# Hybrid decoder layer on one core: query passes 512 wide, top-k behind the heads, softmax as its own step

## The chip, the cores and the metric

One Trainium2 chip, one core of it. The metric is the device time of one execution in microseconds, the median of the runs shown. The kernel is written in Tile: a planner that simulates the program fixes at compile time in which order each engine gets its instructions, by readiness and by the order of the program text, and sets the semaphores. Engines are PE (matrix), DVE (vector), ACT (scalar functions), POOL (GpSimd) and SP (issues DMAs).

## The reference, cut to what matters

```python
h2 = rms_norm(x, g_norm2) * (1 + sc2) + sh2            # 512 tokens x 1024
q = (h2 @ w_query).reshape(T, 8, 2, 128)               # 8 heads, 2 halves
s = einsum('thpd,pkd->thpk', q, sub_keys)              # 128 scores per half
s_top, i_top = top_k(s, 16)                            # first level
cand = s_top[:, :, 0, :, None] + s_top[:, :, 1, None, :]
best, pos = top_k(cand, 16)                            # second level
eidx = take_along(i0 * 128 + i1, pos); g = softmax(best)
a = gelu(einsum('thkd,td->thk', expert_u[eidx], h2))
out = einsum('thk,thkd->td', g * a, expert_v[eidx])    # 16384 experts x 1024
```

In front of it stand the attention and retention groups with their projections, behind it a residual and a last RMSNorm.

## The kernel before, in words

The 512 tokens are four blocks of 128 (`NB`). Blocks 0 to 2 (`DB`) take the expert layer densely: all 16384 experts in 128 chunks, `u_chunk` (line 746) for the inner products and GELU, then `v_load` and `v_mm` (lines 812, 833) for the weighted sum. Their gates are spread into a matrix G over experts by `g_steps` (line 773): 48 steps of four one-hot products on DVE (lines 784 to 787), 16 small matmuls on PE and two copies on ACT each. Block 3 (`GB`) gathers its 128 expert rows per token from HBM with indirect DMAs on POOL (`gather`, line 842).

Products in f32 precision are made of three matmuls (`mm3`, lines 80 to 83): a tile is split into a high part (ACT, line 76) and the rest (line 77, on DVE or POOL, as the caller says).

The order around the change:

- `ORDER` (line 45) lists the steps of the front, here its end: `h0 w1 q0 q1! h1 q2 q3`. `w` is the output projection of a pair of blocks (`wout`, 495), `h` the second norm and transpose of a pair (`h2`, 517), `q` the query of a pair for four heads (`query`, 552). A `!` gives a step high priority. In this stretch SP's DMAs keep the order of the text.
- `query` loads one 128-column piece of `w_query` per head and half, splits it (rest on POOL), makes 24 matmuls of 256 columns, copies the result (line 578), and a tile later makes the scores against the sub-keys (line 561), which are copied behind each head to `Sc` (line 564), over the residual buffers `blk`.
- Behind the front, for b in 0, 1, 2: the u chunks up to `UF[b]` (8 before block 1, 16 before block 2; rest of the split on POOL for chunks under 8, else DVE), then `topk(b)` (line 609). It calls `topk16` (lines 595 to 600) 16 times on 128 scores, adds the 50 candidates per head (lines 625 to 631), calls `topk16` 8 times on those, finds the indices with 16-way comparisons and trees (lines 645 to 655), makes the softmax (lines 656 to 665), and turns indices and gates with three PE transposes (lines 676 to 678).
- Then G steps and u chunks up to 32 alternate, chunks 32 to 35 come behind the last G matmul, and the last stage begins: a v chunk and a u chunk in turn, `R0` = 36 chunks apart. `topk(GB)` is issued at v chunk 2, behind the last one-hot product, and the gathers of block 3 follow in POOL's written order, between the splits of the v chunks.

Of the kernel before, what the change touches and what calls it, by code (L numbers as in the profile page):

```python
# [38 lines left out]
UF = {1: 8, 2: 16}  # L39
# [5 lines left out]
ORDER = "L m0! p1 d3 p2! m1 p3 d4 p4 d2 p5 p6 r0! r1! p7 r2 r3 X0 X1! d5! m2 g! m3 w0 X3 X2 h0 w1 q0 q1! h1 q2 q3"  # L45
# [3 lines left out]
def build(ctx: ExitStack, tc: tile.TileContext, A, out):  # L49
# [502 lines left out]
    def query(pr, hs):  # L552
        bs = (2 * pr, 2 * pr + 1)
# [4 lines left out]
        def scores():  # L558
            qs, h, q, p4 = pend.pop()
            for i in range(2):  # L560
                T.matmul(p4[:, i, q, :], qs[:, i * 128:(i + 1) * 128], subk[:, q, :], start=True, stop=True)
            if q:
                for i, b in enumerate(bs):
                    S.activation(Sc[b][:, h], p4[:, i], AF.Copy)

        for h in hs:
            p4 = acc().rearrange("p (b q k) -> p b q k", b=2, q=2)
            for q in range(2):
                raw = raw_t()
                G.dma_start(raw, A["w_query"][2 * h + q])  # L570
                hi, lo = split(raw, P)
                pa = acc()
# [5 lines left out]
                S.activation(qs[:, :256], pa[:, :256], AF.Copy)  # L578
                if pend:
                    scores()  # L580
                pend.append((qs, h, q, p4))
# [10 lines left out]
    eidx = cp.tile([128, 128], I32, name="eidx")  # L592
    gsm = cp.tile([128, 128], F32, name="gsm")

# [14 lines left out]
    def topk(b, after=None):  # L609
        v1 = tk.tile([128, 8, 2, 16], F32, name="v1", bufs=1)  # L610
        i1 = tk.tile([128, 8, 2, 16], U32, name="i1", bufs=1)
        for h in range(8):
            for q in range(2):
                topk16(v1[:, h, q, :], i1[:, h, q, :], Sc[b][:, h, q, :], 128)
# [5 lines left out]
        cd = tk.tile([128, 8, NC_], F32, name="cd", bufs=1)  # L620
        va, vb = v1[:, :, 0, :], v1[:, :, 1, :]
        o = 0
        for a in range(5):
            n = 16 // (a + 1)
            V.tensor_add(cd[:, :, o:o + n], vb[:, :, :n], va[:, :, a:a + 1].to_broadcast([128, 8, n]))
            o += n
        V.tensor_add(cd[:, :, o:o + 6].rearrange("p h (a b) -> p h a b", a=3),
                     vb[:, :, None, :2].to_broadcast([128, 8, 3, 2]),
                     va[:, :, 5:8, None].to_broadcast([128, 8, 3, 2]))
        o += 6  # L630
        V.tensor_add(cd[:, :, o:o + 8], va[:, :, 8:16], vb[:, :, 0:1].to_broadcast([128, 8, 8]))
        bst = tk.tile([128, 8, 16], F32, name="bst", bufs=1)
        bpos = tk.tile([128, 8, 16], U32, name="bpos", bufs=1)
        for h in range(8):
            topk16(bst[:, h], bpos[:, h], cd[:, h], NC_)
# [19 lines left out]
        tree(ij[:, 1], tm, V)  # L655
        nm = tk.tile([128, 8], F32, name="nmx", bufs=1)
        V.tensor_copy(nm, bst[:, :, 0])
        ee = bst
        V.tensor_sub(ee, bst, nm[:, :, None].to_broadcast([128, 8, 16]))
        S.activation(ee, ee, AF.Exp)  # L660
# [372 lines left out]
```

## Time and profile before

| | us |
|---|---|
| median of 3 runs (lowest to highest) | 1602.66 (1601.04 to 1605.63) |
| the profiled execution, its own time | 1607.23 |
| span of its records | 1605.2 |
| mean granted clock of TensorE | 0.983 of full speed |

Busy shares of the span: PE 94%, weight loads 86%, DVE 80%, POOL 53%, ACT 39%. The profile has one record per instruction; the views used are the page, tables of busy time by stretch, waits, groups by line, and the order in time of one engine. Busy times of neighbouring instructions overlap a little, so a rate is read from start to start.

### The profile page before, as it was taken

The page shows a single profiled execution, that of the slowest core. Times are in us where ns is not written, and L with a number is a line of the kernel's source. Part 1 is how long each engine was busy: PE and PEld are TensorE (multiplying, and loading weights), DVE is VectorE, ACT ScalarE, POOL GpSimd, SP SyncE. Part 2 cuts the span into 40 slices and gives each one's busy share as a digit, 9 for nine tenths or more (in the row PEclk, how much of TensorE's full clock was granted, in tenths as well). Part 3 has the DMA queues.
Part 4 walks back from the last instruction along what each step waited for, and adds up shares of the span by engine and source line. Part 5 has one row for each costly group of instructions (what it writes and reads, how often), then busy time and mean ns, then how long its engine had stood idle before and what let it go on. Part 6 is the DMA issues. An engine that isn't in the chain of part 4 may idle for free.

```text
span 1605.2 us, 24249 instructions
## 1 busy us (share of the span) xinstructions
PE 1515.3 (94%) x8977; PEld 1372.7 (86%) x8977; DVE 1289.7 (80%) x2338; ACT 629.8 (39%) x1015; POOL 849.6 (53%) x498
## 2 busy tenths in 40 slices
PE   7899999998899996999999999999999999999997
PEld 6788987797899995898888999999999999997885
DVE  6865754639989999999898987887887887888953
ACT  4433244444334554443233333333333333333432
POOL 0332742776440000138778877777687777765513
PEclk9999999999899998899999999999999999999998
DMA  9555440554333777959989999889898898899942
GB/s 355 183 186 173 134 159 29 183 163 139 106 118 113 247 234 217 286 185 332 326 312 324 317 333 320 314 305 324 316 330 293 315 322 329 313 321 343 323 159 77
DMA packets 196040, 395.62 MB, mean 246 GB/s; under 512 B 12241, under 2 KB 111569, under 8 KB 195922
## 3 DMA queue, kind: packets, MB, share of 16 engines
q1 hardware_dynamic: 157906, 257.22, 47.6%
q0 software_dynamic: 36864, 134.23, 23.7%
q10 hardware_dynamic: 1152, 2.62, 0.4%
q8 instruction: 70, 1.15, 0.3%
q14 instruction: 48, 0.39, 0.1%
HBM read 364.15 MB, written 29.88 MB: 245 GB/s over the span
## 4 chain that ended last, share of the span: by engine, by line
PE 29%; DMA 20%; issue 20%; DVE 15%; POOL 14%; ACT 1%; POOLq 0%; SPq 0%; DVEq 0%; ACTq 0%
POOL grow L844 8%; DMA grow<-in_expert_v_dram,eidx 8%; DMA grow<-in_expert_u_dram,eidx 6%; POOL vlo L77 5%; PE acc L82 4%; PE acc L81 4%; PE acc L83 4%; DMA vraw<-in_expert_v_dram 3%; PE ab L83 2%; PE ab L81 2%; PE ab L82 2%; DVE lo L77 1%; DMA raw<-in_wadaT_dram 1%; DVE junk L852 1%; DVE ohs L785 1%
## 5 line engine op out<-in xcount | busy, mean ns | idle before, releaser
L77 POOL TENSOR_TENSOR vlo<-vraw,vhi 128x1024 fp32r<-128x1024 f32 x92 | 242.0, 2631 | 293.3 <-ACT vhi L76 291.9
L76 ACT ACTIVATE hi<-raw 128x1024 fp32r<-128x1024 f32 x204 | 216.3, 1060 | 390.2 <-PE ab L82 245.2
L83 PE MATMUL ab<-hh,lo 128*128 128x384 f32 x1024 | 345.9, 338 | 3.6 <-DVE lo L77 2.6
L81 PE MATMUL ab<-hh,hi 128*128 128x384 f32 x1024 | 345.7, 338 | 0.7 <-ACT ga L758 0.6
L82 PE MATMUL ab<-hl,hi 128*128 128x384 f32 x1024 | 344.9, 337 | 0.0
L852 DVE SCALAR_TENSOR_TENSOR junk<-grow,h2n 128x1024 bf16<-128x1024 f32 x128 | 202.0, 1578 | 50.4 <-DMA grow<-in_expert_u_dram,eidx 47.5
L865 DVE SCALAR_TENSOR_TENSOR gacc<-grow,wsl,gacc 128x1024 f32<-128x1024 f32 x126 | 184.4, 1471 | 67.2 <-DMA grow<-in_expert_v_dram,eidx 66.9
L77 DVE TENSOR_TENSOR lo<-raw,hi 128x1024 fp32r<-128x1024 f32 x151 | 204.1, 1352 | 35.5 <-ACT hi L76 35.4
L844 POOL DMA_INDIRECT grow<-in_expert_u_dram,eidx x128 | 180.5, 1410 | 82.0 <-DVE junk L852 33.3
L844 POOL DMA_INDIRECT grow<-in_expert_v_dram,eidx x128 | 190.6, 1489 | 56.7 <-DVE gacc L865 27.8
L83 PEld LDWEIGHTS ab<-hh,lo 128*128 128x128 f32 x1024 | 192.4, 188 | 6.9 <-DVE lo L77 4.6
L81 PEld LDWEIGHTS ab<-hh,hi 128*128 128x128 f32 x1024 | 192.8, 188 | 4.5 <-ACT ga L758 1.0
L82 PEld LDWEIGHTS ab<-hl,hi 128*128 128x128 f32 x1024 | 192.7, 188 | 3.6
L77 POOL TENSOR_TENSOR lo<-raw,hi 128x1024 fp32r<-128x1024 f32 x53 | 133.0, 2512 | 105.4 <-ACT hi L76 104.2
L829 ACT ACTIVATE wh<-wf 128x384 fp32r<-128x384 f32 x110 | 57.5, 524 | 260.5 <-issue 220.8
L76 ACT ACTIVATE vhi<-vraw 128x1024 fp32r<-128x1024 f32 x110 | 115.5, 1050 | 57.2 <-DMA vraw<-in_expert_v_dram 55.0
L82 PE MATMUL acc<-vlo,wh 128*128 128x512 f32 x330 | 129.7, 394 | 6.1 <-POOL vlo L77 6.1
L83 PE MATMUL acc<-vhi,wl 128*128 128x512 f32 x330 | 128.5, 390 | 0.0
L81 PE MATMUL acc<-vhi,wh 128*128 128x512 f32 x330 | 123.2, 390 | 3.2 <-ACT wh L829 1.8
L81 PE MATMUL acc<-hi,hh 128*128 128x256 f32 (+2 forms) x296 | 91.6, 317 | 7.4 <-ACT hi L76 4.9
L830 DVE TENSOR_TENSOR wl<-wf,wh 128x384 fp32r<-128x384 f32 x110 | 88.0, 801 | 11.9 <-ACT wh L829 11.7
L82 PE MATMUL acc<-lo,hh 128*128 128x256 f32 (+2 forms) x296 | 93.8, 317 | 1.5 <-DVE lo L77 0.8
(339 smaller groups left out, 3303.3 us busy)
## 6 DMA issues: line engine op xcount, KB each, us to landing
raw<-in_uT_dram SPq DMA_DIRECT2D x128, 512.0 KB
vraw<-in_expert_v_dram SPq DMA_DIRECT2D x110, 512.0 KB
Gd<-stg SPq DMA_DIRECT2D x12, 2048.0 KB
gtl<-Gd SPq DMA_DIRECT2D x32, 768.0 KB
raw<-in_wadaT_dram SPq DMA_DIRECT2D x40, 512.0 KB
raw<-in_w_query_dram SPq DMA_DIRECT2D x32, 512.0 KB
raw<-in_expert_v_dram SPq DMA_DIRECT2D x18, 512.0 KB
raw<-in_w_out_dram SPq DMA_DIRECT2D x16, 512.0 KB
```

Source lines behind the costliest of these rows:

```text
L76: S.activation(hi[:, :n], raw[:, :n], AF.Copy)
L77: lo_engine.tensor_sub(lo[:, :n], raw[:, :n], hi[:, :n].bitcast(F32))
L81: T.matmul(o, wh, rh, start=start, stop=False, skip_group_check=skip)
L82: T.matmul(o, wh, rl, start=False, stop=False, skip_group_check=skip)
L83: return T.matmul(o, wl, rh, start=False, stop=stop, skip_group_check=skip)
L785: V.tensor_tensor(oh[1], io, bc(ij[:, 0]), op=OP.is_equal)
L829: S.activation(wh, wf, AF.Copy)
L830: V.tensor_sub(wl, wf, wh.bitcast(F32))
L844: P.indirect_dma_start(out=r, out_offset=None, in_=A[table], in_offset=bass.IndirectOffsetOnAxis(ap=eidx[:, s:s + 1], axis=0))
L852: V.scalar_tensor_tensor(jk, r, 1.0, h2n, op0=OP.mult, op1=OP.mult, accum_out=asl[:, s:s + 1])
L865: V.scalar_tensor_tensor(g, r, wsl[:, s:s + 1], g, op0=OP.mult, op1=OP.add)
```

## The change: what it does

The query runs heads 0 and 1 in passes of two blocks, then heads 2 to 4 and 5 to 7 for all four blocks in passes of 512 columns (`QS`); `h1` comes ahead of it. Scores are copied block by block and half by half. Behind each head `level1` makes its first-level calls for the blocks of the pass, block 3 among them; behind head 3 `level2(b, 0)` makes the second level of heads 0 to 3 of blocks 0 to 2. Values and indices of the first level have buffers of their own per block; `bst`, `bpos`, `cd` and the tile `ti` of four 128-column groups lie in `blk`. After the query, per block: the other half of the second level, `topk` (indices only), `gates` (softmax), u chunks up to `UF[b]`, now 2, 7, 12, then `topk_fin`, four transposes and two copies. Chunks 0 to 11 (`NPL`) have their rest made on POOL.

```diff
-UF = {1: 8, 2: 16}
+NPL = 12
+UF = {0: 2, 1: 7, 2: 12}
+QS = (((0, 1), (0, 1)), ((2, 3), (0, 1)), ((0, 1, 2, 3), (2, 3, 4)), ((0, 1, 2, 3), (5, 6, 7)))
-ORDER = "... w0 X3 X2 h0 w1 q0 q1! h1 q2 q3"
+ORDER = "... w0 X3 X2 h0 w1 h1 Q0 Q1 Q2 Q3"
...
         def scores():
-            qs, h, q, p4 = pend.pop()
-            for i in range(2):
-                T.matmul(p4[:, i, q, :], qs[:, i * 128:(i + 1) * 128], subk[:, q, :], start=True, stop=True)
+            qs, h, q = pend.pop()
+            p4 = acc()
+            for i in range(len(bs)):
+                cs = slice(i * 128, (i + 1) * 128)
+                T.matmul(p4[:, cs], qs[:, cs], subk[:, q, :], start=True, stop=True)
+            for i, b in enumerate(bs):
+                last["qa"] = S.activation(Sc[b][:, h, q], p4[:, i * 128:(i + 1) * 128], AF.Copy).ins
             if q:
-                for i, b in enumerate(bs):
-                    S.activation(Sc[b][:, h], p4[:, i], AF.Copy)
+                for b in bs:
+                    level1(b, h)
+                if h == H // 2 - 1:
+                    for b in DB:
+                        level2(b, 0)
...
-                    mm3(pa[:, :256], hi[:, ks], lo[:, ks], hh[:, bs[0]:bs[0] + 2, k, :],
-                        hl[:, bs[0]:bs[0] + 2, k, :], k == 0, k == 7)
+                    mm3(pa[:, :n], hi[:, ks], lo[:, ks], hh[:, bs[0]:bs[0] + len(bs), k, :],
+                        hl[:, bs[0]:bs[0] + len(bs), k, :], k == 0, k == 7)
...
+    def level1(b, h):
...
+        for q in range(2):
+            topk16(v1[:, h, q, :], i1[:, h, q, :], Sc[b][:, h, q, :], 128)
...
+    def level2(b, half):
+        bst, bpos, cd, _ = spare(b)
...
+        for a in range(5):
+            n = 16 // (a + 1)
+            V.tensor_add(cd[:, hs, o:o + n], vb[:, :, :n], va[:, :, a:a + 1].to_broadcast([128, 4, n]))
...
+        for h in range(4 * half, 4 * half + 4):
+            topk16(bst[:, h], bpos[:, h], cd[:, h], NC_)
...
+    def gates(b, after=None):
+        ti = tin[b]
+        ee = ti[:, 3].rearrange("p (h k) -> p h k", h=8)
+        with tc.issue_after(after) if after else ExitStack():
+            S.activation(ee, ee, AF.Exp)
...
+        gh = tk.tile([128, 16, 8], F16, name="pb", bufs=1).rearrange("p k h -> p (k h)")
+        V.tensor_scalar(gh, gg, GSC, None, op0=OP.mult)
+        V.scalar_tensor_tensor(ti[:, 3], gg, GSC, gh, op0=OP.mult, op1=OP.subtract)
+        V.tensor_copy(ti[:, 2], gh)
+
+    def topk_fin(b, after):
+        ti = tin[b]
+        with tc.issue_after(after):
             p = ob()
-            T.transpose(p[:, :128], iF[:, 0], ident)
-            T.transpose(p[:, 128:256], iF[:, 1], ident)
-            T.transpose(p[:, 256:384], gg, ident)
+            for q in range(4):
+                T.transpose(p[:, q * 128:(q + 1) * 128], ti[:, q], ident)
...
     for b in DB:
-        while nu < UF.get(b, 0):
-            u_chunk(nu, P if nu < 8 else V)
+        level2(b, 1)
+        topk(b)
+        gates(b, last["qa"])
+        while nu < UF[b]:
+            u_chunk(nu, P if nu < NPL else V)
             nu += 1
-        topk(b, last.get("u"))
+        topk_fin(b, last["u"])
...
             with tc.issue_after(last["o"]):
+                level2(GB, 0)
+                level2(GB, 1)
                 topk(GB)
+                gates(GB)
```

## Rows read from the trace of the kernel before

**Rows 1.** The page, part 1: busy us (share of the span) xinstructions

```profile
PE 1515.3 (94%) x8977; PEld 1372.7 (86%) x8977; DVE 1289.7 (80%) x2338; ACT 629.8 (39%) x1015; POOL 849.6 (53%) x498
```

**Rows 2.** Busy us by stretch (us from, to; length; engines; clock; DMA), last stage

```profile
700.00:800.00 100.00, 96.36 (x481) 85.49 (x480) 86.65 (x105) 32.27 (x44) 73.11 (x43) 1.00 0.86 300
800.00:1000.00 200.00, 195.69 (x991) 177.54 (x990) 180.04 (x206) 71.37 (x97) 157.68 (x90) 1.00 0.92 322
```

**Rows 3.** The same table, from the query to the G build's end

```profile
308.00:320.00 12.00, 11.23 (x91) 10.60 (x89) 4.22 (x5) 7.27 (x12) 10.83 (x8) 1.00 0.63 230
308.00:361.00 53.00, 52.23 (x441) 51.53 (x440) 19.33 (x104) 27.05 (x49) 40.52 (x20) 1.00 0.53 175
361.00:443.00 82.00, 67.76 (x521) 64.74 (x520) 80.84 (x370) 35.64 (x71) 45.77 (x19) 0.94 0.38 122
443.00:493.00 50.00, 48.27 (x276) 47.28 (x276) 42.84 (x147) 16.70 (x25) 15.48 (x6) 1.00 0.37 124
493.00:580.00 87.00, 85.69 (x687) 81.06 (x685) 86.03 (x192) 44.03 (x72) 0.00 (x0) 1.00 0.62 194
580.00:651.00 71.00, 53.32 (x543) 48.17 (x543) 69.09 (x113) 37.92 (x68) 0.00 (x0) 0.85 0.74 225
```

**Rows 4.** Waits of DVE, 308 to 651: us in total, times, longest

```profile
DVE v L596 <- ACT blk L564: 28.1, 7, 5.1
...
DVE i L597 <- PE ob L677: 3.0, 2, 2.2
```

**Rows 5.** DVE in order of time (start, us): first-level calls, last one-hot product

```profile
320.28 0.49 DVE L596 MAX8 v<-blk 128x8 f32<-128x128 f32 x2 [2.50 <-ACT blk L564]
...
322.44 0.29 DVE L600 FIND_INDEX8 i<-v,blk 128x8 uint32<-128x128 f32 x1
...
649.52 0.69 DVE L787 TENSOR_TENSOR ohs<-ohs,gt 128x1024 f16<-128x1024 f16 x1
```

**Rows 6.** DVE by line, 308 to 651 (five), then 652 to 711 (two): busy, mean ns

```profile
L77 DVE TENSOR_TENSOR lo<-raw,hi 128x1024 fp32r<-128x1024 f32 x25 | 30.7, 1229 | 6.0 <-ACT hi L76 6.0
L605 DVE TENSOR_TENSOR t4k<-t4k 128x1024 f16<-128x1024 f16 (+2 forms) x27 | 22.6, 860 | 0.2
...
L646 DVE TENSOR_TENSOR t4k<-t4k,dd 128x2048 f16<-128x2048 f16 x3 | 7.7, 2550 | 0.0
...
L537 DVE TENSOR_SCALAR w<-tp,mod 128x256 f32<-128x256 f32 x8 | 3.9, 531 | 0.0
L542 DVE TENSOR_TENSOR hl<-w,hh 128x256 fp32r<-128x256 f32 x8 | 3.9, 510 | 0.0
...
L605 DVE TENSOR_TENSOR t4k<-t4k 128x1024 f16<-128x1024 f16 (+2 forms) x9 | 4.0, 462 | 0.1
...
L646 DVE TENSOR_TENSOR t4k<-t4k,dd 128x2048 f16<-128x2048 f16 x1 | 1.2, 1204 | 0.0
```

**Rows 7.** DVE, then POOL, in order of time in topk(0)

```profile
388.15 0.18 DVE L625 TENSOR_TENSOR cd<-v 128x24 f32<-128x24 f32 x1
...
388.56 3.22 DVE L646 TENSOR_TENSOR t4k<-t4k,dd 128x2048 f16<-128x2048 f16 x1
...
388.12 5.91 POOL L77 TENSOR_TENSOR lo<-raw,hi 128x1024 fp32r<-128x1024 f32 x2 [1.70 <-ACT hi L76]
```

**Rows 8.** PE in order of time: 512 wide (output projection), score matmuls of the query

```profile
298.07 0.39 PE L81 MATMUL acc<-hi,hh 128*128 128x512 f32 x1
298.30 0.39 PE L82 MATMUL acc<-lo,hh 128*128 128x512 f32 x1
...
322.77 0.60 PE L561 MATMUL acc<-subk,w 128*128 128x128 f32 x4
...
326.05 0.61 PE L561 MATMUL acc<-subk,w 128*128 128x128 f32 x4
```

**Rows 9.** Waits of PE, 400 to 420

```profile
PE ob L676 <- DVE i L674: 9.6, 1, 9.6
```

**Rows 10.** POOL in order of time: the first gather

```profile
710.91 1.90 POOL L844 DMA_INDIRECT grow<-in_expert_u_dram,eidx  x1 [26.01 <-DVE eidx L670]
```

More of the change, by code (lines that the diff above doesn't have):

```diff
@@ L550, in h2, with query @@
                     S.dma_start(h2d[:, kp * 256:(kp + 1) * 256], hn[:, :256])
-    def query(pr, hs):
-        bs = (2 * pr, 2 * pr + 1)
+    def query(bs, hs):
+        n = len(bs) * 128
         for b in bs:
@@ L607, in tree, with spare, topk @@
         e.tensor_add(dst, t[:, 0], t[:, 1])
[L609 to L614, printed above, removed]
+    lv, tin = {}, {}
+    def level1(b, h):
+        if b not in lv:
+            if b == 1:
+                t = lv[0][2]
+            else:
+                t = (tk if b == GB else fr).tile([128, 512 if b == GB else 1024], F32,
+                                                 name=("fhi", None, "flo", "v1")[b], bufs=1)
+            o = 512 * (b == 1)
+            v = t[:, o:o + 256].rearrange("p (h q a) -> p h q a", h=8, q=2)
+            i = t[:, o + 256:o + 512].bitcast(U32).rearrange("p (h q a) -> p h q a", h=8, q=2)
+            lv[b] = v, i, t
+        v1, i1, _ = lv[b]
+        for q in range(2):
+            topk16(v1[:, h, q, :], i1[:, h, q, :], Sc[b][:, h, q, :], 128)
+    def spare(b):
+        f = blk[b].rearrange("p a c -> p (a c)")
+        return (f[:, 0:128].rearrange("p (h k) -> p h k", h=8),
+                f[:, 128:256].bitcast(U32).rearrange("p (h k) -> p h k", h=8),
+                f[:, 256:256 + H * NC_].rearrange("p (h n) -> p h n", h=8), f[:, 1024:1536])
+    def level2(b, half):
+        bst, bpos, cd, _ = spare(b)
+        v1 = lv[b][0]
+        hs = slice(4 * half, 4 * half + 4)
+        va, vb = v1[:, hs, 0, :], v1[:, hs, 1, :]
+        o = 0
+        for a in range(5):
+            n = 16 // (a + 1)
+            V.tensor_add(cd[:, hs, o:o + n], vb[:, :, :n], va[:, :, a:a + 1].to_broadcast([128, 4, n]))
+            o += n
+        V.tensor_add(cd[:, hs, o:o + 6].rearrange("p h (a b) -> p h a b", a=3),
+                     vb[:, :, None, :2].to_broadcast([128, 4, 3, 2]),
+                     va[:, :, 5:8, None].to_broadcast([128, 4, 3, 2]))
+        o += 6
+        V.tensor_add(cd[:, hs, o:o + 8], va[:, :, 8:16], vb[:, :, 0:1].to_broadcast([128, 4, 8]))
+        for h in range(4 * half, 4 * half + 4):
+            topk16(bst[:, h], bpos[:, h], cd[:, h], NC_)
+    def topk(b):
+        bst, bpos, _, ti = spare(b)
+        i1 = lv[b][1]
         di = tk.tile([128, 2, 17, 8], F16, name="di", bufs=1)
@@ L688, in mla_all @@
         mix_T(b, 0, mla(b))
+    last = {}
     yms = [None] * NB
@@ L729, in build @@
             h2(n)
-        elif o == "q":
-            query(n // 2, range(4 * (n % 2), 4 * (n % 2) + 4))
+        elif o == "Q":
+            query(*QS[n])
         hp.close()
@@ L737, in build @@
     gas = {}
-    last = {}
     def u_load(c):
@@ L874, in build @@
             left -= 1
-        u_chunk(c, P if c < 8 else V)
+        u_chunk(c, P if c < NPL else V)
     held = [u_load(c) for c in range(R0 - HOLD, R0 - HOLD + 3)]
@@ L886, in build @@
     row_bc(5, gt2)
+    eidx = lp.tile([128, 128], I32, name="eidx")
+    gsm = lp.tile([128, 128], F32, name="gsm")
     vacc += [acc() for _ in range(3)] + [tpb() for _ in range(2)] + [ob()]
```

52 lines of the change are left out of this document (15 added, 37 removed).

## The prediction

> **What bounds the kernel now.** I read four views, from coarse to fine. The page's first part: PE is busy for 1515 of 1605 us [rows 1], so the time of a stage is PE's work unless something starves it. The table of stretches shows where that happens. From 700 us on PE is busy for all but 8.0 us of 300 [rows 2], and that stage (u chunks and v chunks together) has a fixed amount of PE work: it ends a fixed time after it starts. So the question is when it starts. It waits for the last step of the G build, whose last one-hot product starts at 649.5 [rows 5], and the G build hangs on DVE: from 361 to 651 DVE is busy 80.8 of 82, 42.8 of 50, 86.0 of 87 and 69.1 of 71 us [rows 3], while PE stands idle for 17.7 us of the last of these. Ahead of that, from 308 to 361, the picture is turned round: PE is full (52.2 of 53) and DVE idles for 33.7 us. The waits of DVE say on what: 28.1 us on the copies of the query scores [rows 4]. All in all DVE is busy 298.1 of the 343 us from 308 to 651 and idle 44.9. So the start of the last stage moves by the change of DVE's work before 651, plus the change of its idle time. PE's share of the query is not the term.
>
> **The change, part by part** (on the start of the last stage, in us).
>
> *Block 3's first level comes forward.* Before, all of `topk(3)` ran behind the G build. Now its 16 first-level calls run behind the query heads. Two calls take from 320.28 to 322.65 including their last instruction, 2.4 us [rows 5], so one is 1.21 and 16 are **+19.4** on DVE ahead of 651. The other three blocks' calls only move.
>
> *Split engine.* `NPL` gives POOL the low halves of chunks 0 to 11 instead of 0 to 7: four fewer on DVE at 1.23 [rows 6], **-4.9**.
>
> *Second level in halves, softmax apart.* Seven additions of `cd` become fourteen per block, 21 more in three blocks. One took 0.18 [rows 7], so 21 are 3.8 at most, less where neighbours overlap. `gates` adds three small copies per block and drops one, some 2 in all. I take **+3** for both (bounds 1 and 6; near the middle, since back-to-back records overlap).
>
> *Query passes.* A 256-wide tile repeats every 3.27 us with its four score matmuls, which span 0.6 [rows 8]. A 512-wide matmul starts 0.23 after the one before it [rows 8], 24 of them take 5.6; with eight score matmuls a tile is 6.5, twice 3.27. So PE gains nothing: 8 x 3.27 + 12 x 6.5 = 104 us either way, against 32 x 3.27. Weight loads, splits (20 instead of 32) and loads of `w_query` (20 instead of 32, on SP) fall away where neither ACT nor the DMA engines were full: 27.1 of 53 us, share 0.53 [rows 3]. Score copies become 64 narrow ones on ACT for 32; even at 0.4 each they are 26 us in 104 and hide in ACT's idle half. I put all of this at nothing; without that cover it would be those 26 us.
>
> *DVE's idle time.* Built by hand from those periods, with `h2(1)` now ahead of the query. Up to 320 as before: 12.0 - 4.2 = 7.8 idle [rows 3] (the first call is at 320.28 [rows 5]). Q0 and Q1 are eight tiles, 26.2 us of PE, plus some 6 for the transposes of `h2(1)` and the wait for its last quarter: PE starts Q2 at 340. Meanwhile DVE has 16 first-level calls (19.4) and 7.8 of `h2(1)` (L537, L542) [rows 6], which now meets POOL's splits; I allow 4 for that, and DVE runs dry at 320 + 31 = 351. The first four-block head is complete after three tiles and its copies, 340 + 19.5 + 1 = 360.5: 9 idle. A head feeds DVE 8 x 1.21 = 9.7 per 13.0 of PE, so 3.3 more before the next one. Then the first half of the second level (three blocks, about 4.5 each) falls due behind head 3 and DVE has a backlog past the end of the query, near 418. That makes 20. Of the 11.2 idle after 361 before, the 3.0 in which an index tile waited for PE's transposes [rows 4] goes (each block has its own tile now), and I leave 6. So 26 for 44.9: **-19**. Bounds: 14 (always fed from 361 on) and 45 (nothing gained).
>
> *POOL beside DVE.* The second step of `topk` slows when POOL splits: L646 took 3.22 us at 388.56, beside two splits that took 5.91 [rows 7], and 1.2 after 652, where POOL stood mostly idle [rows 6]. In 308 to 651 the two largest groups carry 7.7 - 3 x 1.2 = 4.1 and 22.6 - 3 x 4.0 = 10.6 of such excess [rows 6]; with the smaller ones I estimate 25. Before, blocks 0 and 1 met splits of the query at 2.4 in 3.27 us; now only chunks 0 to 11 are beside block 0 and part of block 1, and the first halves of the second level run among splits every 6.5 us. I take **-4** (bounds: -25, none left; +10, four more splits at 2.4 in the way).
>
> The rule for this is on the Trainium skill's page SBUF — State Buffer, section "SBUF: two separate sides": a GpSimd instruction and a DVE instruction with two SBUF inputs exclude each other for a whole instruction. The rows of L646 agree; by the rule the loss goes with the number of splits that fall beside `topk`, about as many as before, which would make this term 0 instead of -4 and the sum 4 us worse.
>
> *Waits added.* `topk_fin` puts four transposes on PE behind the chunk that `UF` names. If DVE is late, the following chunks queue behind them, as for 9.6 us before [rows 9]. Each chunk's split waits in turn, but PE had 17.7 us to spare in 580 to 651 [rows 3], so a wait of that size costs nothing; beyond it, it counts in full. `Exp` in `gates` waits behind the last score copy on ACT, ahead of GELUs that have time.
>
> *Sum:* 19.4 - 4.9 + 3 - 19 - 4 = **-5.5**.
>
> *After the start.* The indices came so late that POOL, in its written order, stood 26.0 us in front of the first gather, at 710.9 [rows 10]. With 19.4 less to do there DVE gives the indices earlier, and v splits no longer pile up behind. PE idles 8.0 us in 700 to 1000 [rows 2]; I take half, **-4** (bounds 0 and -8).
>
> The profiled execution took 1607.23 us (span 1605.2), 4.57 above the median of the runs. 1607.2 - 9.5 = 1597.7; less 4.57 that is **1593** against 1602.66.
>
> **Rivals.**
>
> 1. *DVE is not fed earlier.* The place is the first four-block head: if its scores come late (Q1 waiting longer for `h2(1)`, or the planner putting heads behind other PE work), DVE's idle stays at 45 while block 3's 19.4 us are in front of the G build. Then 19.4 - 4.9 + 3 - 4 = +13.5, and +9.5 with the 4 behind the start: **1612**. It decides from about 40 us of idle on, since 14 more than my 26 is a loss of 4.8. For it: the wide pass doubles the time to a head's scores, and DVE before needed only 4.9 us a head. Against: the two heads in two-block passes give DVE 19.4 us of work to bridge this gap.
>
> 2. *POOL takes it back.* The loss beside POOL does not shrink by 4 but grows by 4 or 5, because `h2(1)`, the half levels and `topk` of two blocks all meet POOL's splits: 1593 + 9 = **1602**, no change. For it: 25 us lost that way before. Against: 40 splits in the query and chunks become 32.
>
> 3. *PE was bound by weights.* In 308 to 361 weight loads are busy 51.5 of 53 us [rows 3]. The wide passes need 480 instead of 768 of the query's loads, and with 2.8 us for 24 of them one costs at most 0.12: PE would gain up to 288 x 0.12 = 34 us, DVE's idle would fall to some 10 (the 7.8 up to 320 and little else), and it ends at 1593 - 16 = **1577**. That loads, not matmuls, measure TensorE is what the Trainium skill says (Perfetto Trace Analysis, "Identifying the Most-Contended Engine"). Against: 0.23 per 512-wide matmul is as long per column [rows 8].
>
> **How the numbers follow.** About 0.3%, 4.8 us, is what a measurement of this kernel can tell from no change. Forecast 0.49, rival 1 0.22, rival 2 0.23, rival 3 0.06. Faster: 0.49 + 0.06 = 0.55. Same 0.23. Slower 0.22. The forecast's own range is 1587 to 1598, from idle times of 20 to 30. The whole range reaches down to rival 3 and to contention nearly gone, 1577, and up to rival 1, 1612; what lies outside is both bad ends together (idle 45 and +10 beside POOL), or both good ends.
>
> **What would show it.** DVE's idle from the start of the query to the last one-hot product: 26, against 45. Block 3's first level ahead of that product, and the product near 645 instead of 650. Query tiles 6.5 us apart; PE waiting on DVE at least as long as before near the end of the G build. Two-input DVE instructions beside splits still at two to three times their length. First gather less than 40 us behind the last one-hot product, instead of 710.9 - 649.5 = 61. It is wrong if query tiles come much under 6.5, if DVE idles 40 or more, or if PE loses more time in the last stage than it did.

## The result, and the profile after

| | before | after |
|---|---|---|
| median of four runs, same chip | 1603.91 us (1601.04 to 1605.63) | 1587.53 us (1585.24 to 1613.96) |
| ratio, with 95% interval | | **0.9866** (0.9833 to 0.9899) |
| the same kernel on another chip (run 9) | 1609.80 us | 1592.16 us, 0.9901 (0.9881 to 0.9920) |
| profiled execution, span | 1607.23, 1605.2 us | 1585.5, 1583.7 us |

The ratio leaves out the one disturbed run of after, the 1613.96; the median of the other three is 1585.50. The kernel is faster: by 21 us by the first ratio, by 18 by these medians, by 16 by the second ratio. The forecast was 9.5 us. The page of after, part 1 (busy us, share of the span, instructions), beside [rows 1]:

```profile
PE 1507.8 (95%) x8692; PEld 1358.3 (86%) x8692; DVE 1276.3 (81%) x2369; ACT 622.1 (39%) x1027; POOL 824.2 (52%) x490
```

The table of stretches of after (us from, to; length; PE, PE's weight loads, DVE, ACT, POOL busy; clock; DMA), in the cuts of [rows 2, 3] as far as they are the same:

```profile
308.00:361.00 53.00, 47.67 (x321) 42.87 (x320) 34.02 (x171) 24.26 (x57) 29.63 (x14) 0.97 0.43 141
361.00:443.00 82.00, 82.00 (x434) 72.71 (x433) 77.12 (x524) 31.21 (x74) 33.74 (x14) 1.00 0.27 90
443.00:493.00 50.00, 36.26 (x184) 35.06 (x183) 49.62 (x146) 18.03 (x25) 16.27 (x6) 0.86 0.24 75
493.00:580.00 87.00, 85.89 (x722) 80.38 (x720) 84.84 (x137) 48.02 (x79) 0.00 (x0) 1.00 0.70 210
...
700.00:800.00 100.00, 100.00 (x510) 91.31 (x510) 93.95 (x109) 35.61 (x49) 77.67 (x46) 1.00 0.91 328
800.00:1000.00 200.00, 200.00 (x1021) 182.85 (x1020) 162.22 (x196) 71.41 (x98) 150.84 (x87) 1.00 0.88 311
```

DVE's idle time in 308 to 361 fell from 33.7 to 19.0 us. PE's idle time moved out of 361 to 443 into 443 to 493, where it stands behind DVE's top-k. And from 700 to 1000 PE has no gap at all, with 1531 matmuls in these 300 us where before had 1472 [rows 2].

The waits of DVE in after, 308 to 644 (us in total, times, longest), against [rows 4], and DVE in order of time, against [rows 5]:

```profile
DVE fhi L601 <- ACT blk L567: 13.3, 8, 4.0
DVE flo L601 <- ACT blk L567: 5.6, 4, 3.1
```

```profile
325.37 0.49 DVE L601 MAX8 fhi<-blk 128x8 f32<-128x128 f32 x2 [1.17 <-ACT blk L567]
...
642.68 0.68 DVE L826 TENSOR_TENSOR ohs<-ohs,gt 128x1024 f16<-128x1024 f16 x1
```

The waits on score copies are 18.9 us for 28.1. The last one-hot product starts at 642.7 instead of 649.5: 6.8 us of the 21.5 that the span lost. The other 14.7 lie behind it. The waits of PE in after, 644 to the end, are all that is left there, 2.8 us. The longest stands at 1428.8 us, far behind block 3's top-k:

```profile
PE acc L83 <- ACT ga L868: 1.9, 1, 1.9
PE ab L83 <- ACT gb L794: 0.5, 1, 0.5
PE acc L85 <- DVE wl L869: 0.4, 1, 0.4
```

And POOL in order of time shows the first gather 40.0 us behind that product, against [rows 10]: it waited 4.8 us instead of 26.0.

```profile
682.68 1.23 POOL L883 DMA_INDIRECT grow<-in_expert_u_dram,eidx  x1 [4.77 <-DVE eidx L705]
```

### The profile page after: what moved, and what is told of

Read it like the earlier page. It is cut to its first block, busy times and chain, and to the rows that moved or that the text cites. A ratio compares the mean times of both kernels' runs of the same rounds, so it can differ in the third digit from the quotient of the medians.

```text
span 1583.7 us, 23659 instructions
## 1 busy us (share of the span) xinstructions
PE 1507.8 (95%) x8692; PEld 1358.3 (86%) x8692; DVE 1276.3 (81%) x2369; ACT 622.1 (39%) x1027; POOL 824.2 (52%) x490
## 4 chain that ended last, share of the span: by engine, by line
PE 49%; DMA 16%; DVE 15%; issue 12%; POOL 8%; ACT 1%; SPq 0%; POOLq 0%; DVEq 0%; ACTq 0%
DMA grow<-in_expert_v_dram,eidx 8%; PE ab L85 6%; PE ab L83 6%; PE ab L84 6%; PE acc L83 5%; PE acc L85 5%; PE acc L84 5%; POOL grow L883 4%; DMA vraw<-in_expert_v_dram 4%; PE tp L85 2%; PE tp L84 2%; PE tp L83 2%; POOL vlo L79 2%; PE ob L85 1%; PE ob L84 1%
## 5 line engine op out<-in xcount | busy, mean ns | idle before, releaser
L83 PE MATMUL ab<-hh,hi 128*128 128x384 f32 (+2 forms) x1184 | 404.4, 342 | 7.0 <-ACT ga L794 6.5
L85 PE MATMUL ab<-hh,lo 128*128 128x384 f32 (+2 forms) x1184 | 403.8, 341 | 2.8 <-POOL lo L79 2.0
L84 PE MATMUL ab<-hl,hi 128*128 128x384 f32 (+2 forms) x1184 | 401.8, 339 | 0.0
L78 ACT ACTIVATE hi<-raw 128x1024 fp32r<-128x1024 f32 x192 | 203.7, 1061 | 405.5 <-PE ab L84 245.6
L891 DVE SCALAR_TENSOR_TENSOR junk<-grow,h2n 128x1024 bf16<-128x1024 f32 x128 | 193.2, 1509 | 64.2 <-DMA grow<-in_expert_u_dram,eidx 63.3
L79 DVE TENSOR_TENSOR lo<-raw,hi 128x1024 fp32r<-128x1024 f32 x147 | 212.3, 1445 | 32.9 <-ACT hi L78 32.8
L83 PEld LDWEIGHTS ab<-hh,hi 128*128 128x128 f32 x1184 | 224.1, 189 | 15.1 <-ACT ga L794 7.2
L85 PEld LDWEIGHTS ab<-hh,lo 128*128 128x128 f32 x1184 | 223.8, 189 | 8.0 <-POOL lo L79 2.4
L84 PEld LDWEIGHTS ab<-hl,hi 128*128 128x128 f32 x1184 | 224.0, 189 | 7.1
L883 POOL DMA_INDIRECT grow<-in_expert_u_dram,eidx x128 | 177.5, 1387 | 50.4 <-DVE junk L891 21.7
L79 POOL TENSOR_TENSOR lo<-raw,hi 128x1024 fp32r<-128x1024 f32 x45 | 110.5, 2456 | 146.9 <-ACT hi L78 146.8
L869 DVE TENSOR_TENSOR wl<-wf,wh 128x384 fp32r<-128x384 f32 x110 | 89.6, 814 | 13.2 <-ACT wh L868 12.0
```

Source lines behind the costliest of these rows:

```text
L78: S.activation(hi[:, :n], raw[:, :n], AF.Copy)
L79: lo_engine.tensor_sub(lo[:, :n], raw[:, :n], hi[:, :n].bitcast(F32))
L83: T.matmul(o, wh, rh, start=start, stop=False, skip_group_check=skip)
L84: T.matmul(o, wh, rl, start=False, stop=False, skip_group_check=skip)
L85: return T.matmul(o, wl, rh, start=False, stop=stop, skip_group_check=skip)
L869: V.tensor_sub(wl, wf, wh.bitcast(F32))
```

## The experiments

Theory for the gain behind the start: POOL works in its written order. Before, it stood 26 us in front of the first gather, the v splits queued behind it, and a v chunk came late in a stage that PE bounds. Rival: DVE's own load in block 3's top-k made the v chunks late. Theory for the start: DVE's work and idle time, as the prediction summed them. Rivals: the parts of the change taken singly.

Runs 1 to 4 shared a chip, 5 to 8 a second, 9 to 12 a third; a ratio is to the kernel before on the same chip. "Start" is the start of the last one-hot product. "Front" is the time to it from the last addition of the output projection on POOL, where the part that all kernels share ends. "Stage" is the time from the start to the end of the last matmul, "PE idle" PE's idle time in it, "low" the part of it in which TensorE's granted clock was 0.50, the lower of its two levels (1.2 and 2.4 GHz). "Matmuls" is PE's count in the first 400 us of the stage, "idle" DVE's idle time from 308 us to the start. All but the ratio are of the one profiled execution, which lies up to 6.5 us off the median of its kernel's runs (run 7).

| run | ratio (95%) | start | front | stage | PE idle | low | matmuls | idle |
|---|---|---|---|---|---|---|---|---|
| before | 1 | 649.5 | 340.0 | 944.1 | 13.0 | 3.4 | 1988 | 44.9 |
| after | 0.9866 (0.9833 to 0.9899) | 642.7 | 333.5 | 929.2 | 2.9 | 0.4 | 2054 | 28.5 |
| 1 before, late gathers | 0.9938 (0.9923 to 0.9954) | 648.1 | 339.5 | 940.0 | 8.9 | 13.6 | 2037 | 44.8 |
| 2 after, block 3's first level back | 0.9943 (0.9924 to 0.9962) | 641.6 | 333.8 | 949.3 | 14.2 | 20.2 | 1997 | 43.5 |
| 3 as 2, late gathers | 0.9900 (0.9879 to 0.9921) | 641.6 | 333.8 | 939.9 | 9.1 | 9.9 | 2011 | 43.6 |
| 4 after, gathers one chunk later | 0.9862 (0.9842 to 0.9881) | 643.9 | 334.8 | 935.1 | 7.0 | 3.4 | 2042 | 30.0 |
| 5 before, own buffers | 1.0016 (1.0000 to 1.0033) | 651.3 | 342.8 | 946.5 | 13.2 | 10.2 | 1997 | 44.2 |
| 6 as 5, late gathers | 0.9981 (0.9966 to 0.9997) | 654.8 | 342.9 | 936.5 | 6.2 | 6.8 | 2031 | 45.8 |
| 7 after, second level in three parts | 0.9916 (0.9901 to 0.9931) | 640.8 | 334.8 | 931.4 | 3.8 | 3.4 | 2052 | 16.9 |
| 8 after, no chunk's rest on POOL | 0.9925 (0.9910 to 0.9939) | 641.3 | 332.2 | 943.8 | 12.0 | 7.8 | 2006 | 31.8 |
| 9 after again | 0.9901 (0.9881 to 0.9920) | 644.3 | 335.0 | 934.2 | 5.9 | 3.4 | 2035 | 30.0 |
| 10 after, narrow | 0.9919 (0.9899 to 0.9940) | 646.4 | 336.8 | 935.1 | 6.3 | 6.8 | 2030 | 25.5 |
| 11 after, wide throughout | 0.9906 (0.9884 to 0.9928) | 642.3 | 334.0 | 936.0 | 6.8 | 6.2 | 2049 | 30.2 |
| 12 before, three parts | 0.9962 (0.9945 to 0.9979) | 653.4 | 342.3 | 936.3 | 6.2 | 7.7 | 2028 | 55.1 |

Profiles that share a front (before and 1; after, 4 and 9; 5 and 6) differ by 1.4, 1.6 and 3.5 us in the start. A part of this is older than the change: that last addition begins between 305.9 (run 7) and 311.9 us (run 6). In "front" the same profiles differ by 0.5, 1.4 and 0.1 us, so the front is the better measure; by it the change is worth 4.5 to 6.5 us. In the stage the two profiles of one kernel (after, 9) differ by 5, so no smaller differences are read.

The clock has a part in the stages. PE in order of time, run 2, at granted clock 0.50 and at full clock: 512 columns start 0.43 and 0.23 us apart, so 1 us of "low" costs about 0.47. This stretch, 10.2 us from 1440.0 on, began while PE stood 7.7 us for one operand.

```profile
1447.83 0.63 PE L84 MATMUL acc<-lo,ga 128*128 128x512 f32 x1
1448.26 0.63 PE L83 MATMUL tp<-hi,ga 128*128 128x512 f32 x1
...
1452.19 0.39 PE L84 MATMUL acc<-vlo,wh 128*128 128x512 f32 x1
1452.42 0.39 PE L85 MATMUL acc<-vhi,wl 128*128 128x512 f32 x1
```

Stage less PE idle less 0.47 of low is 925 to 930 us in all fourteen profiles: an estimate, and a check that little else sets the length of a stage. Where an expectation names a length of the stage, it counts to a matmul about 3 us before the last.

### Behind the start: runs 1 to 4

**Run 1**, the kernel before with its gathers four v chunks later.

```diff
-        if c < LEAD:
+        if c < LEAD + 4:
             continue
         credit += CR[0] if c + R0 < NK else CR[1]
```

> The kernel before, with block 3's gathers started four v chunks later (chunk 6 for chunk 2); its top-k stays where it was, so DVE has the same work at the same place. Theory (POOL's written order: the first gather stands 26 us for the indices, the splits of the next v chunks queue behind it, and a v chunk comes 12 us or more late in a stage that PE bounds): no split waits behind a gather, PE is full from 662 on, and the time falls by 10 to 14 us, to about 1591. Rival (DVE's own work in block 3's top-k, 58 us behind the last one-hot product, is what makes the v chunks late): no gain, within 3 us of the kernel before.

Measured 0.9938, 10 us; PE's first 400 us hold 2037 matmuls for 1988. POOL in order of time, run 1: it makes the next chunks' splits first, three of which stand here, and waits 3.5 us for the indices instead of 26.0 [rows 10].

```profile
686.34 2.40 POOL L77 TENSOR_TENSOR vlo<-vraw,vhi 128x1024 fp32r<-128x1024 f32 x1 [1.32 <-ACT vhi L76]
696.77 2.94 POOL L77 TENSOR_TENSOR vlo<-vraw,vhi 128x1024 fp32r<-128x1024 f32 x1 [8.03 <-ACT vhi L76]
702.86 4.74 POOL L77 TENSOR_TENSOR vlo<-vraw,vhi 128x1024 fp32r<-128x1024 f32 x1 [3.14 <-ACT vhi L76]
...
717.36 1.23 POOL L844 DMA_INDIRECT grow<-in_expert_u_dram,eidx  x1 [3.50 <-DVE eidx L670]
```

So the written order cost before some 10 us, with DVE's top-k of block 3 unchanged and the mean granted clock of both kernels' runs at 0.980: the theory, at the lower end of its range.

**Run 2**, the kernel after with block 3's first level back behind the G build.

```diff
                 for b in bs:
-                    level1(b, h)
+                    if b != GB:
+                        level1(b, h)
...
             with tc.issue_after(last["o"]):
+                for h in range(H):
+                    level1(GB, h)
                 level2(GB, 0)
```

> The kernel after, with block 3's 16 first-level calls put back behind the G build. Theory: 19.4 us of DVE work leave the front, but a part of them filled time in which DVE would have waited for score copies, so the last one-hot product comes 8 to 14 us earlier than in the kernel after (629 to 635 for 642.7); block 3's indices come later behind it, POOL again stands more than 20 us in front of the first gather, and the last stage gives back 10 to 14 us: between 3 us faster and 6 us slower than the kernel after, 1584 to 1594. Rival 1 (the place of block 3's first level does not matter for the last stage): 8 to 14 us faster than the kernel after, about 1576. Rival 2 (DVE is fed late, and the calls cost nothing in the front): the last one-hot product stays near 643, the last stage loses, about 1598.

Measured 0.9943, 13 us over run 4, which has the front of after. The 19.4 us left the front and its end moved by 1.1 us only (front 333.8 for 333.5 in after): rival 2. The table of stretches says why. After first, then run 2:

```profile
308.00:443.00 135.00, 129.67 (x754) 115.59 (x753) 111.14 (x693) 55.48 (x131) 63.37 (x28) 0.99 0.33 110
443.00:493.00 50.00, 36.26 (x184) 35.06 (x183) 49.62 (x146) 18.03 (x25) 16.27 (x6) 0.86 0.24 75
493.00:610.00 117.00, 115.89 (x1009) 108.09 (x1008) 112.82 (x179) 64.96 (x109) 0.00 (x0) 1.00 0.72 216
610.00:642.00 32.00, 19.38 (x217) 17.15 (x215) 32.00 (x54) 15.86 (x29) 0.00 (x0) 0.80 0.84 239
```

```profile
308.00:443.00 135.00, 128.62 (x741) 114.58 (x741) 97.14 (x587) 54.62 (x130) 62.21 (x27) 0.99 0.33 109
443.00:493.00 50.00, 39.30 (x198) 37.18 (x197) 49.62 (x130) 15.36 (x23) 17.74 (x6) 0.86 0.25 84
493.00:610.00 117.00, 114.19 (x981) 106.09 (x980) 112.22 (x175) 63.95 (x108) 0.00 (x0) 0.99 0.71 213
610.00:642.00 32.00, 19.27 (x236) 16.77 (x234) 31.51 (x53) 16.42 (x31) 0.00 (x0) 0.88 0.81 231
```

DVE's busy time (third of the busy figures) is 14.0 us shorter in the first stretch, while PE runs the query, and 1.1 us in the other three together. From 443 on DVE is as full as before. Its waits on score copies in run 2 took the time (18.9 us in after):

```profile
DVE fhi L602 <- ACT blk L567: 25.5, 11, 4.6
DVE flo L602 <- ACT blk L567: 7.5, 4, 3.8
```

And behind the start the old loss is back: POOL, run 2, waits 27.2 us for the indices, and the 400 us hold 1997 matmuls. It is not all of the 13 us: run 2's stage has 20.2 us at the lower clock level for 3.4 in run 4, by the estimate above some 8 us, and over all of their runs the mean granted clock was 0.978 for 0.982.

```profile
705.34 1.20 POOL L884 DMA_INDIRECT grow<-in_expert_u_dram,eidx  x1 [27.20 <-DVE eidx L706]
```

**Run 3**, run 2 with the edit of run 1 (`LEAD + 4`).

> As the run before, and the gathers start four v chunks later. Theory: it keeps the earlier last one-hot product (629 to 635) and loses nothing behind it, since no v split waits behind a gather: 8 to 14 us faster than the kernel after, 1574 to 1580. Rival (DVE's longer top-k behind the G build holds the v chunks up by itself): no faster than with the gathers in their old place, 1584 to 1594.

Measured 0.9900: 7 us better than run 2, still 6 over run 4. The wait of POOL is gone and gives 7 us; 6 are left. That DVE's longer top-k makes these 6, as the rival has it, is not shown. The waits of PE in run 3, 642 to 900, do name a product for the v chunks (`wf` on DVE, then `wh` on ACT) that came late:

```profile
PE acc L83 <- ACT wh L869: 3.8, 1, 3.8
PE ab L85 <- DVE lo L79: 1.8, 2, 1.0
```

But in the whole stage PE idles only 2 us more than in run 4, and 6.5 us more at the lower clock level are worth another 3; over all of their runs the mean granted clock was 0.979 for 0.982.

**Run 4**, the kernel after with `LEAD + 1` in the same line.

> The kernel after, with the gathers started one v chunk later. Theory: of the wait for the indices 4.8 us are left in the kernel after, and PE is already full from 662 on, so there is at most the 1.9 us of PE waits left in the stage: within 3 us, 1585 to 1588. Rival (each us of that wait still counts in the stage): 4 to 5 us faster, 1582 to 1583.

Measured 0.9862 against 0.9866: nothing, as the theory had it. But the wait only fell from 4.8 to 3.6 us, with one v split more ahead of it, so the run says little about what the rest of it costs.

### The front: runs 5, 12, 7 and 8

**Run 5**, the kernel before with first-level buffers of their own.

```diff
-        v1 = tk.tile([128, 8, 2, 16], F32, name="v1", bufs=1)
-        i1 = tk.tile([128, 8, 2, 16], U32, name="i1", bufs=1)
+        if b == GB:
...
+        else:
+            t = lv[0] if b == 1 else fr.tile([128, 1024], F32, name="flo" if b else "fhi", bufs=1)
+            lv[b] = t
+            o = 512 * (b == 1)
+            v1 = t[:, o:o + 256].rearrange("p (h q a) -> p h q a", h=8, q=2)
+            i1 = t[:, o + 256:o + 512].bitcast(U32).rearrange("p (h q a) -> p h q a", h=8, q=2)
```

> The kernel before, with buffers of their own for the first-level values and indices of blocks 0 to 2, and nothing else changed: query passes 256 wide, block 3's top-k and the gathers where they were. Theory A (the front's gain is that the first level no longer waits for the top-k of the block before to let go of its buffer; pass width and order are not needed): DVE's idle time from 308 us to the last one-hot product falls from 44.9 to about 25 us, that product comes 14 to 20 us earlier (630 to 636 for 649.5), and behind it the stage takes as long as in the kernel before: 14 to 20 us faster than before, as fast as the kernel after or a little faster. Theory B (the wide passes, the order of the heads, or the splits given to POOL make the gain): within 4 us of the kernel before.

Measured 1.0016, start 651.3: no gain, theory B so far (the front is even 2.8 us longer than that of before). But the waits of ACT and PE in run 5 (308 to the start) show a new one: ACT stood 24.3 us in front of three Exp, up to 11.0 at a time, for DVE's top-k, and copies of the query queued behind them.

```profile
ACT bst L669 <- DVE bst L668: 24.3, 3, 11.0
```

```profile
PE acc L561 <- ACT w L578: 9.5, 5, 7.9
```

**Run 6**, run 5 with `LEAD + 4`.

> As the run before, and the gathers start four v chunks later, as in the first run of this study, where that gave 10 us. If front and last stage are two separate terms, the two gains add: 8 to 11 us less than with the buffers alone, some 25 us less than the kernel before and 5 us or more less than the kernel after. If they are not (an earlier start only makes DVE's top-k of block 3 weigh more on the v chunks, as 8 us stayed behind in the third run), the two together give less than 5 us over the buffers alone.

Measured 0.9981, 5.6 us under run 5, stage 936.5 for 946.5. The late gathers' gain is there without any change of the front; that it adds to a gain in the front could not be seen, as there was none.

**Run 12**, run 6 with Exp behind the last score copy.

```diff
-                    S.activation(Sc[b][:, h], p4[:, i], AF.Copy)
+                    last["qa"] = S.activation(Sc[b][:, h], p4[:, i], AF.Copy).ins
...
-        S.activation(ee, ee, AF.Exp)
+        with tc.issue_after(last["qa"]):
+            S.activation(ee, ee, AF.Exp)
```

> The kernel before with three parts and no wide pass: buffers of their own for the first level (as in run 5), the gathers four v chunks later (as in run 1), and the softmax's Exp behind the last score copy on ACT, as the kernel after has it. In run 5 ACT stood 24.3 us in three Exp, up to 11.0 at a time, with copies of the query and splits queued behind, and PE waited 9.5 us on those copies. Theory A (the buffers would have paid, but for Exp in ACT's queue): those waits are gone, the last one-hot product comes at 640 to 646, the stage behind it takes 930 to 937, and the whole is 12 to 20 us faster than before, within 5 us of the kernel after. Theory B (the wide passes with their order of heads make the front's gain): the last one-hot product stays within 3 us of 649.5, and the gain is the late gathers' 5 to 10 us alone.

Measured 0.9962, start 653.4, front 342.3 for 340.0: no gain in the front, theory B again, if 0.9 us past its 3 us in the start. PE's wait on those copies is no longer among its larger ones, and DVE's idle time is the longest of all, 55.1 us. Its largest wait in run 12:

```profile
DVE flo L598 <- ACT blk L566: 22.9, 4, 7.8
```

`flo` holds block 2. Here the query still runs blocks 0 and 1 to the end and then blocks 2 and 3, so DVE works off the first pair and then stands for the second. In after every head from the third on brings all four blocks.

That is not the only reading. PE, too, stood in this query: in the middle of a tile it waited 11.0 us for the index transposes of `topk(0)`, as it did for 9.6 us in before [rows 9], and the first of the four waits for block 2 ends at 427.5, 10 us behind it. PE in order of time, run 12:

```profile
417.37 0.47 PE L688 MATMUL ob<-ident,i 128*128 128x128 f32 x1 [11.01 <-DVE i L686]
```

In after these transposes stand behind the query. Runs 5 and 12 left them in it, and no run moved them alone.

**Run 7**, the kernel after with the second level of heads 0 and 1 behind head 1 (`level2` takes a range of heads).

```diff
+                if h == 1:
+                    for b in bs:
+                        if b != GB:
+                            level2(b, 0, 2)
                 if h == H // 2 - 1:
                     for b in DB:
-                        level2(b, 0)
+                        level2(b, 2, 4)
```

> The kernel after, with the second level of heads 0 and 1 of blocks 0 to 2 behind head 1 instead of behind head 3: 24 calls, some 7 us of DVE work, come into the stretch from 340 to 380 us, where DVE stands idle for 13.7 of 40 us. Theory (work that is pulled into that gap leaves the backlog behind the query, and the backlog sets the start): the last one-hot product 4 to 7 us earlier, 636 to 639, and 3 to 6 us faster than the kernel after. Rival (the front is not set by DVE's backlog: in the second run 19.4 us taken out of the front moved its end by 1 to 2 us only): within 2 us of the kernel after.

Measured 0.9916, start 640.8. That is 2 to 3 us earlier than in the profiles with after's front, but so was the end of the output projection: the front, 334.8, is that of runs 4 and 9. DVE's idle time fell from 28.5 to 16.9 (over the front, from 27.8 to 19.0), but its busy time to the start rose from 306.2 to 315.8. The additions that make the candidates ate the gain, in groups of DVE from 308 us to the start, after first, then run 7:

```profile
L645 DVE TENSOR_TENSOR blk<-fhi 128x32 f32<-128x32 f32 (+4 forms) x20 | 7.7, 408 | 0.0
...
L645 DVE TENSOR_TENSOR blk<-flo 128x32 f32<-128x32 f32 (+4 forms) x10 | 1.6, 171 | 0.0
```

```profile
L649 DVE TENSOR_TENSOR blk<-fhi 128x16 f32<-128x16 f32 (+7 forms) x30 | 15.7, 547 | 0.0
...
L649 DVE TENSOR_TENSOR blk<-flo 128x16 f32<-128x16 f32 (+7 forms) x15 | 6.0, 423 | 0.0
```

Fifteen more of them, and each up to 0.55 us long on the mean where one took 0.18 [rows 7]: together 21.7 for 9.3 us. They stand among the query's splits on POOL. No gain in time; the rival.

**Run 8**, the kernel after with `NPL = 0`.

```diff
-NPL = 12
+NPL = 0
```

> The kernel after, with the rest of chunks 0 to 11 made on DVE instead of POOL: 12 instructions of 1.13 us, 13.6 us more on DVE, all of them behind the last query pass, where DVE has a backlog. Theory (DVE's work there counts in full; little of POOL's contention is lost): the last one-hot product 9 to 14 us later, 652 to 657, and 9 to 14 us slower than the kernel after. Rival 1 (POOL's splits held DVE's two-input instructions up by about as much as they saved): between 4 us faster and 4 us slower. Rival 2 (DVE does not set the start): within 2 us, with DVE's idle time down by 13 us.

The start came at 641.3, not at 652 to 657, with 32 splits on DVE to the start (38.9 us) for 20 (24.4): rival 1. A part of what paid for the 14.5 us is in three groups of DVE, 308 to 642, of after and of run 8:

```profile
L610 DVE TENSOR_TENSOR t4k<-t4k 128x1024 f16<-128x1024 f16 (+2 forms) x27 | 13.9, 535 | 0.0
L680 DVE TENSOR_TENSOR t4k<-pb,kc 128x2048 f16<-128x2048 f16 x3 | 5.9, 1961 | 0.1
L675 DVE TENSOR_TENSOR t4k<-t4k,kc 128x2048 f16<-128x2048 f16 x3 | 5.8, 1942 | 0.0
```

```profile
L610 DVE TENSOR_TENSOR t4k<-t4k 128x1024 f16<-128x1024 f16 (+2 forms) x27 | 12.0, 459 | 0.0
L680 DVE TENSOR_TENSOR t4k<-pb,kc 128x2048 f16<-128x2048 f16 x3 | 3.7, 1226 | 0.1
L675 DVE TENSOR_TENSOR t4k<-t4k,kc 128x2048 f16<-128x2048 f16 x3 | 3.7, 1217 | 0.0
```

The largest single one is a copy of `gates` (line 708), 5.0 us for three in after and 0.7 in run 8. Taken together, DVE's busy time to the start went from 306.2 to 301.5 us while 14.5 us of splits were added. The time, 0.9925, is not better, and this profile's stage was 943.8; why that is, stays open (PE's clock was 0.89 in its first 20 us, it waited 6.1 us on `lo` of DVE, and the profiled execution, 1598.71 us, is the longest of the six, 5.0 over their median).

### The width of the passes: runs 9 to 11

**Run 9** is the kernel after, unchanged.

> The kernel after itself, unchanged, on the chip of the next three, as their measure. Both theories: 0.984 to 0.990 of the kernel before, last one-hot product 7 us or so earlier than there (642 to 644), the stage behind it near 926 to 932.

Measured 0.9901, at the upper edge; start 644.3.

**Run 10**, heads 2 to 7 in passes of two blocks. (`ORDER` names the fourteen passes; the first half of the second level stays behind head 3 of the second pair.)

```diff
-QS = (((0, 1), (0, 1)), ((2, 3), (0, 1)), ((0, 1, 2, 3), (2, 3, 4)), ((0, 1, 2, 3), (5, 6, 7)))
+QS = (((0, 1), (0, 1)), ((2, 3), (0, 1))) + tuple((p, (h,)) for h in range(2, 8) for p in ((0, 1), (2, 3)))
...
-                if h == H // 2 - 1:
+                if h == H // 2 - 1 and GB in bs:
```

> The kernel after, with heads 2 to 7 in passes of two blocks (256 columns) instead of four; the heads come in the same order, pair after pair. Theory (width is worth nothing by itself: 0.23 us for 512 columns against half of that for 256, and what feeds DVE is the order of the heads): last one-hot product within 3 us of the kernel after, time within 4 us of it. Rival 1 (PE is bound by weight loads, 288 more at up to 0.12 us): 20 to 34 us slower than the kernel after. Rival 2 (the 12 more splits on POOL, 2.4 us each, hold up DVE and the query): 5 to 12 us slower.

Measured 0.9919, 3 us over run 9, start 646.4: within the theory's 4 us. Rival 1 falls. Rival 2 asked for 5 us at least; the medians are 4.6 apart, so its low end is not quite excluded. PE in order of time, the score matmuls that close a query tile, in after and in run 10, 6.41 and 3.27 us apart:

```profile
355.98 1.05 PE L565 MATMUL acc<-subk,w 128*128 128x128 f32 x8
362.39 1.05 PE L565 MATMUL acc<-subk,w 128*128 128x128 f32 x8
```

```profile
395.22 0.61 PE L565 MATMUL acc<-subk,w 128*128 128x128 f32 x4
398.49 0.61 PE L565 MATMUL acc<-subk,w 128*128 128x128 f32 x4
```

**Run 11**, four blocks throughout.

```diff
-QS = (((0, 1), (0, 1)), ((2, 3), (0, 1)), ((0, 1, 2, 3), (2, 3, 4)), ((0, 1, 2, 3), (5, 6, 7)))
+QS = (((0, 1, 2, 3), (0, 1, 2, 3)), ((0, 1, 2, 3), (4, 5, 6, 7)))
```

> The kernel after, with heads 0 and 1 for all four blocks as well: no two-block passes, 512 columns throughout. Theory (the two-block heads bridge the wait for the second half of the norm and for the first four-block head): PE stands some 6 to 10 us for the norm of blocks 2 and 3 before the first pass, the query ends that much later, DVE's first call comes 10 us or more later, and the last one-hot product comes 5 to 10 us later: 5 to 10 us slower than the kernel after. Rival (runs 2, 5 and 7: DVE's and PE's gaps in the query are slack): within 3 us of the kernel after.

Measured 0.9906, the same as run 9. DVE's first call does come later, 331.5 for 325.4 in after, and the start does not (642.3): the rival.

```profile
331.53 0.49 DVE L601 MAX8 fhi<-blk 128x8 f32<-128x128 f32 x2 [6.00 <-ACT blk L567]
```

No kernel here is shown to beat the kernel after; run 4's interval lies within that of after.

## Why the prediction was right, and where it was not

The direction and the start were right: -6.8 us for the sum's **-5.5**, with idle 28.5 for the 26 forecast. As bookkeeping the sum held: DVE's work to the start rose by 9.6 us (296.6 to 306.2) for the 13.5 summed, and its idle time fell by 16.4 for 19. As a mechanism it did not, as run 2 shows below, so that the start came out is in part luck. The whole was too small by 6 to 12 us, and the step that failed is a term that was mis-sized: **"After the start", -4**, with bounds 0 and -8.

*After the start.* The stage shortened by 14.9 us in the first pair of profiles, by 9.9 with run 9's. The mechanism was the one named (the indices come earlier, splits no longer pile up behind), but I sized it from PE's 8.0 us of idle time [rows 2]. The same rows give 1472 matmuls in 300 us of before; after makes 1531. At 300 us for 1531, the missing 59 are 11.6 us of work: part of the loss stood inside PE's busy time. And it was idle time of a part only: in the whole stage it fell from 13.0 to 2.9. With the gathers' wait taken away the stages of runs 1, 6 and 12 average 937.6; with it, before and run 5 average 945.3; after and run 9 average 931.7. So of 13.6 us some 8 are POOL's written order. The other 6 are not shown to be DVE's shorter top-k behind the start, the part that the experiments call the rival. Runs 1, 6 and 12 stood 9.4 us on the mean at the lower clock level, after and 9 only 1.9, which is some 3.5 of the 6. Of 2.7 us more of PE idle time, 1.6 lie in one wait between 1429 and 1447 us, far behind the top-k. That leaves about 1 us.

*Block 3's first level, +19.4, and DVE's idle time, -19.* The sum of the two came out, but they are not two terms. Run 2 takes the calls away: idle rises to 43.5, and the start moves by 1.1 us. PE's query sets when the scores come; DVE has slack until the last of them, and calls put there cost nothing but the few behind the last scores. My hand-built schedule was wrong in detail as well: DVE's first call came at 325.4, not at 320.28, and the planner fed it half by half, not head by head.

*Rival 1 (DVE is not fed earlier).* It did not happen, but not for my reason. The two-block heads that were to bridge the gap are not needed (run 11), and idle time alone was no price: run 2 has 43.5 us of idle and an earlier start, though without block 3's calls in front, so the rival's own case was not tried. (14 us more than 26 is a loss of 4.5, not 4.8; and by [rows 5] the two calls end at 322.73, not 322.65. Neither moves the sum.)

*Split engine, -4.9, and POOL beside DVE, -4.* The first was wrong as a term of its own: run 8 puts 12 splits on DVE and the start does not come later. DVE's work without splits fell from 306.2 - 24.4 to 301.5 - 38.9, by 19.2 us; that is 1.6 us of waiting for each of the 12 splits that left POOL, and DVE needs 1.2 for one. This is rival 2's mechanism; it ate this edit, not the whole change. The rule of the Trainium skill's page SBUF — State Buffer, "SBUF: two separate sides", by which the loss goes with the splits that fall beside `topk`, agrees with run 8 and would have given 0 for the -4. For the -4 itself, though, the groups of before, after and run 8 give some -6, an estimate: the trees fell by 8.8 us and the first product (line 646, [rows 6]) by 4.0, other groups beside POOL by 1.4 in sum, and 8.5 us came on with the additions and copies of the next but one paragraph.

*Query passes, nothing.* Right: tiles 6.41 us apart for the 6.5 forecast, and run 10 loses 3 to 5 us with 288 more weight loads, where rival 1 of that run wanted 20 or more. Rival 3 fell: the busy weight loads of [rows 3] bounded nothing. The Trainium skill (Perfetto Trace Analysis, "Identifying the Most-Contended Engine") takes the busy share of weight loads for a measure of TensorE's headroom. Here 51.5 of 53 us did go with a full PE, but 288 loads fewer freed no time, so the share does not say that the loads are the limit; the measurement decides. What did change is the end of the query, which the prediction set aside: its last score matmuls start at 424.9 us for 439.8, and the 9.6 us for which PE stood in it [rows 9] are gone.

*Second level in halves, +3; waits added, nothing.* Neither was tried alone. In after the additions took 14.1 us for 8.3 in before, and the three copies of `gates` 6.4 for the 1.3 of the one that fell away: +10.9, outside the bounds. In run 8, with no chunk's split on POOL, it is 9.9 and 2.1, so +2.4. The +3 was the bare price; 8.5 us more are splits of POOL that stood in the way, up to 2.4 us for one of the copies (DVE, after, 308 to 642), and run 7 shows the same for thirds.

```profile
L708 DVE TENSOR_SCALAR pb<-blk 128x128 f16<-128x128 f32 x2 | 4.8, 2392 | 0.0
```

The added waits are in the trace of after (PE 7.5 us on the transposes, ACT 9.1 on Exp) and lie in 443 to 493, where PE idles 13.7 us in all; whether they set anything there was not tried.

*What stays open* is which part made the start 6.8 us earlier (the front 4.5 to 6.5 us shorter). It was not the width (run 10), the bridging heads (run 11), block 3's calls (run 2), the splits given to POOL (run 8) or the buffers, alone or with Exp moved (runs 5, 12). What is left is the order of the heads, all four blocks together, with the halved second level and the new `UF`, and the place of the index transposes, behind the query instead of in it. The 22.9 us of run 12 speak for the order, its 11.0 us for the place; neither was tried by itself. Nor was one more line of the change, which has the query's products written to the PSUM buffers `ab` instead of `acc`, from which the scores take theirs. That starts hardly move in runs 2, 7 and 8 fits the stretch 493 to 610 of after, where PE is busy 115.9 and DVE 112.8 of 117 us: relieving one meets the other. That is argued, not shown.

## What to carry to other kernels

Work that follows a paced feeder is priced by what lies behind the feeder's last delivery, not by its sum; adding it to one term and the lost idle time to another counts the same microseconds twice. A wait in an engine's written order is charged with what is queued behind it, so put the waiting instructions behind those that are ready, and size the loss by the count of instructions in a fixed stretch against a full one: busy time hides part of it. Moving work to an engine that holds up another is only priced by a profile with and without it. And before a few microseconds are put down to a cause, take out what the clock and the part ahead of the change did.

## What the hardware showed unexpectedly

A DVE instruction with one small input also stood for a whole POOL split. In after, DVE's copy of 128x8 values began 0.16 us behind a split and took 2.33 us; in run 8, with no split beside it, it took 0.15. After's DVE, its POOL, and run 8's DVE, in order of time:

```profile
450.85 2.33 DVE L687 COPY nmx<-blk 128x8 f32<-128x8 f32 x1
```

```profile
450.69 2.46 POOL L79 TENSOR_TENSOR lo<-raw,hi 128x1024 fp32r<-128x1024 f32 x1 [8.61 <-ACT hi L78]
```

```profile
454.88 0.15 DVE L687 COPY nmx<-blk 128x8 f32<-128x8 f32 x1
```

I had counted on two-input instructions only.
